# High and low activations side by side in one 512-column product, and a filter product that contracts over all 128 rows

## The chip, the cores and the metric

The kernel runs on one core of a Trainium2 chip. The core has five engines that run side by side and wait for each other by semaphores: TensorE (PE, matrix products into the PSUM banks; its weight loads are a row of their own, PEld), VectorE (DVE), ScalarE (ACT), GpSimd (POOL, which does not reach PSUM) and SyncE (SP, which issues the DMAs). The metric is device time of one execution in microseconds (us), lower is better.

## The reference

Two layers of an encoder trunk on one sequence of 256 tokens of width 1024, all in float32. Shortened to what the products are:

```python
for l in range(DEPTH):                                  # DEPTH = 2
    u = rms_norm(x, norm_mix_pre[l])
    proj = u @ w_in[l]                                  # [q,k,v: 4608 columns | Hyena v,x1,x2: 3072 columns]
    y_att = dilated_attention(q, k, v) @ w_o_attn[l]
    hv, hx1, hx2 = split(short_conv(proj[..., 4608:], conv_w, conv_b), 3)
    filt = implicit_filters(...)                        # (sin MLP @ w3) * decay
    z = hx1 * bidir_fft_conv(hv, filt[0], filt[1], hy_bias[0])
    z = hx2 * bidir_fft_conv(z, filt[2], filt[3], hy_bias[1])
    y_hy = z @ w_o_hyena[l]
    gates = sigmoid(u @ w_gate[l] + b_gate[l])          # 2 x 1024 columns
    x = x + rms_norm((gates0 * y_att + gates1 * y_hy) @ w_out[l], norm_mix_post[l])
    u = rms_norm(x, norm_ffn_pre[l])
    a, b = split(u @ w_gate_up[l], 2)                   # 2 x 2816 columns
    x = x + rms_norm((silu(a) * b) @ w_down[l], norm_ffn_post[l])
```

## The kernel before

Weights stream in as pieces of 128 rows of SBUF by 768 or 1024 float32 values, in one fixed order (`order`). Every piece is split into a high and a low part (`whi`, `wlo`): ACT copies the rounded value (`hi_of`, L86), DVE or, for every fifth piece, POOL subtracts it (`lo_of`, L89). Activations are split in the same way. A float32 product is then three passes that add up in one PSUM bank: high weights by high activations, high by low, low by high (`mm3`, L80 to L83). `piece()` keeps three pieces split ahead of the one in use.

A layer's products come in this order: queries, keys and values of the head slots 0 and 1 by rows (384 columns a matmul); 24 Hyena column pieces (`col_proj`, then `shortconv`); 16 gate pieces (`col_proj`, then a sigmoid); head slots 2 and 3; 8 pieces of `w_o_hyena` and 4 of `w_o_attn` (their results are multiplied by the gates, L750 and L766, and the sum is split into `MH`, `ML`); `w_out` by rows (`row_proj`); then the FFN: 8 pieces by rows, 38 by columns (`col_proj`, `Silu`, product, L794 to L800), and `w_down` by rows. `col_proj` runs eight blocks `k` of 128 rows, each an `mm3` with 256 columns (all tokens).

The three by-columns kinds of product have their activations in two tiles each: `UH`, `UL` for u, `zh`, `zl` for the Hyena result, `OTH`, `OTL` for attention.

Beside the pieces runs side work, in generators that `tick()` advances one step after each piece: the filters (`filter_chunk`, 16 of them, eight for a layer: `sd`, `sh`, `sl`, then two pairs of products with `gst`, then `dd`, `dl` and the transforms into `K`), attention (`attend`) and the convolutions (`conv`). `gst` holds 128 rows: the high part of 64 values above the low part of the same 64; the weights `w3` stand twice, in rows 0 to 63 and 64 to 127.

The order on PE is the order in which the code is written. On ACT, DVE, POOL and SP a scheduler sets the order when the program is built, except in the stretches marked `ordered()` between phases. PSUM has eight banks of 512 float32 columns, all in one ring (`acc`).

Of the kernel before, what the change touches and what calls it, by code (L numbers as in the profile page):

```python
# [39 lines left out]
# piece numbers in the packed weights  # L40
# [4 lines left out]
def trunk(tc, nc, a, out):  # L45
# [4 lines left out]
    with es:  # L50
# [82 lines left out]
        shared = [True]  # Pool takes some of the splitting  # L133
        count = [0, 0]  # pieces in wp; pieces split
# [95 lines left out]
        def sine(o, pre, n, par, c0):  # L230
            """o = sin(fr * (pre + b)), the argument brought into [-pi, pi] first."""
# [34 lines left out]
        def new_filter(l):  # L266
            """Tiles of the two filters' spectra and the jobs that fill them."""
# [14 lines left out]
        def filter_chunk(l, v, cc, K, fd, shared):  # L282
# [14 lines left out]
            late = l == 1 and cc == 2  # queued ahead of the layer's start, not to run in it  # L297
# [7 lines left out]
            lo_of(sl[:64], sd[:64], sh[:64], nc.gpsimd)  # L305
# [3 lines left out]
            for e in range(2):  # L309
                h = acc()  # L310
                mm(h, gst[l][:, e, :], sh, True, False)
                mm(h, gst[l][0:64, e, :], sl[0:64], False, True)
# [11 lines left out]
            for s in range(2):  # cosine transform of the sum, sine transform of the difference  # L324
# [45 lines left out]
        def add_to_x(i, t, r):  # L370
            """x += rms_norm * gain for one token tile."""
# [20 lines left out]
        def to_cols(i, u, U):  # L392
            """The transpose of one token tile of u, in parts."""
            for h in range(2):
# [27 lines left out]
        def rows_of(U, o, i, pc, kk, n):
            """Two of the eight row blocks of u[tile i] @ w for a piece of n columns."""
# [82 lines left out]
        def start(U, second, at=0):  # L506
            """The first 2 * 384 columns of a phase by rows, the first token tile ahead of the second."""
# [452 lines left out]
```

## Time and profile before

| | |
|---|---|
| runs | 1122.82 us median of 3 (1122.39 to 1125.14) |
| span of the profiled execution | 1117.8 us, first to last instruction; the median of the runs is 5.0 us above it |
| busy | PE 1094.3 us (98%), PEld 1035.3, DVE 704.1 (63%), ACT 557.1 (50%), POOL 412.5 (37%) |
| matmuls | 7624 in the trace, each with a weight load of its own |
| transfers | 187.21 MB, mean 167 GB/s |

Matmuls are pipelined and the end of one is modelled, so that PE's busy time says only that a matmul was under way; how much one costs is read from the distance between the starts of two. The profile's times are counted from the start of its span. In the trace the layer-0 mixer reaches to about 370 us, its FFN to about 575, the layer-1 mixer to about 918 and its FFN to the end.

### The profile page before, as it was taken

The numbers are of one execution on the slowest core, as the hardware profiler recorded it, in microseconds if no ns is written. First come the engines' busy times: TensorE is split into PE (matmuls) and PEld (weight loads), VectorE is DVE, ScalarE is ACT, GpSimd is POOL, SyncE is SP. The second block draws the span as 40 slices with busy tenths as digits, with TensorE's granted clock in tenths as the row PEclk, the third lists the DMA queues.
The fourth block names the chain that finished last, engine by engine and source line by source line (L and its number), as shares of the span: only waits on it lengthen the run. The fifth ranks groups of instructions, "written<-read, shape, count | busy, mean of one in ns | idle before, by whom it ended". The sixth has DMA issues, their size and how long they took to land.

```text
span 1117.8 us, 19545 instructions
## 1 busy us (share of the span) xinstructions
PE 1094.3 (98%) x7624; PEld 1035.3 (93%) x7624; DVE 704.1 (63%) x1128; ACT 557.1 (50%) x852; POOL 412.5 (37%) x499
## 2 busy tenths in 40 slices
PE   8999999999999999999999999999999999999997
PEld 7889999999998899999879899999999978999986
DVE  6789875556557756665474877865545676454554
ACT  6555564444645644454455564454355455544442
POOL 3665133468614224211125714455645221111110
PEclk9999999999999999999999999999999999999999
DMA  8565534444545655555655444444355466456662
GB/s 295 170 228 187 153 127 136 129 127 125 153 143 183 198 189 169 185 175 183 198 195 166 137 165 145 133 152 129 121 169 186 151 207 207 137 185 182 201 199 79
DMA packets 59878, 187.21 MB, mean 167 GB/s; under 512 B 6919, under 2 KB 9353, under 8 KB 59786
## 3 DMA queue, kind: packets, MB, share of 16 engines
q1 hardware_dynamic: 59786, 185.96, 52.1%
q8 instruction: 60, 0.98, 0.4%
q14 instruction: 32, 0.26, 0.1%
HBM read 184.89 MB, written 1.05 MB: 166 GB/s over the span
## 4 chain that ended last, share of the span: by engine, by line
PE 85%; DVE 5%; DMA 3%; POOL 2%; ACT 2%; issue 1%; SPq 0%; DVEq 0%; POOLq 0%; ACTq 0%
PE acc L78 83%; DVE wlo L89 2%; DMA gain<-in_gains_dram 1%; DMA raw<-in_wa_dram 1%; PE acc L617 1%; ACT whi L86 1%; ACT jk L352 1%; DVE X L373 1%; DMA raw<-in_wq_dram 1%; POOL GT L767 1%; PE acc L397 1%; PE acc L548 1%; PE acc L647 1%; POOL wlo L89 1%; DVE dd L315 0%
## 5 line engine op out<-in xcount | busy, mean ns | idle before, releaser
L86 ACT ACTIVATE whi<-raw 128x1024 fp32r<-128x1024 f32 (+1 forms) x352 | 345.4, 990 | 399.1 <-PE acc L78 297.4
L89 DVE TENSOR_TENSOR wlo<-raw,whi 128x1024 fp32r<-128x1024 f32 (+1 forms) x291 | 346.6, 1197 | 232.7 <-ACT whi L86 220.6
L78 PE MATMUL acc<-UH,whi 128*128 128x256 f32 x1248 | 357.6, 287 | 0.0
L78 PE MATMUL acc<-UH,wlo 128*128 128x256 f32 x1248 | 353.7, 283 | 0.0
L78 PE MATMUL acc<-UL,whi 128*128 128x256 f32 x1248 | 353.5, 283 | 0.0
L89 POOL TENSOR_TENSOR wlo<-raw,whi 128x1024 fp32r<-128x1024 f32 (+1 forms) x61 | 137.2, 2248 | 408.4 <-ACT whi L86 396.6
L78 PEld LDWEIGHTS acc<-UH,whi 128*128 128x128 f32 x1248 | 239.6, 192 | 2.5 <-issue 1.7
L78 PEld LDWEIGHTS acc<-UL,whi 128*128 128x128 f32 x1248 | 239.6, 192 | 0.0
L78 PEld LDWEIGHTS acc<-UH,wlo 128*128 128x128 f32 x1248 | 239.5, 192 | 0.0
L78 PE MATMUL acc<-wlo,UH 128*128 128x384 f32 x448 | 152.3, 340 | 6.0 <-DVE wlo L89 3.8
L78 PE MATMUL acc<-whi,UH 128*128 128x384 f32 x448 | 153.6, 343 | 0.0
L78 PE MATMUL acc<-whi,UL 128*128 128x384 f32 x448 | 150.8, 337 | 0.0
L78 PE MATMUL acc<-whi,hs 128*128 128x512 f32 x352 | 109.1, 390 | 0.0
L78 PEld LDWEIGHTS acc<-wlo,UH 128*128 128x128 f32 x448 | 84.8, 189 | 10.6 <-DVE wlo L89 6.9
L78 PEld LDWEIGHTS acc<-whi,UH 128*128 128x128 f32 x448 | 84.8, 189 | 2.0 <-issue 1.1
L78 PEld LDWEIGHTS acc<-whi,UL 128*128 128x128 f32 x448 | 84.6, 189 | 0.2 <-DVE UL L89 0.2
L78 PEld LDWEIGHTS acc<-whi,hs 128*128 128x128 f32 x352 | 66.1, 188 | 13.7
L78 PE MATMUL acc<-wlo,hs 128*128 128x512 f32 x176 | 68.7, 390 | 0.2 <-DVE wlo L89 0.2
L799 DVE TENSOR_TENSOR HF<-acc,silu 128x256 f32<-128x256 f32 x38 | 16.1, 424 | 52.5 <-PE acc L78 52.5
L359 POOL TENSOR_SCALAR nv<-ss 128x1 f32<-128x1 f32 x16 | 4.8, 300 | 107.5 <-ACT jk L352 107.5
L78 PEld LDWEIGHTS acc<-wlo,hs 128*128 128x128 f32 x176 | 33.1, 188 | 7.3 <-DVE wlo L89 0.7
L565 POOL TENSOR_TENSOR t<-t 128x256 f32<-128x256 f32 x32 | 23.5, 737 | 38.9 <-DVE t L562 38.0
(164 smaller groups left out, 1695.8 us busy)
## 6 DMA issues: line engine op xcount, KB each, us to landing
raw<-in_wa_dram SPq DMA_DIRECT2D x240, 512.0 KB, 3.6
raw<-in_wq_dram SPq DMA_DIRECT2D x96, 384.0 KB, 3.1
raw<-in_wg_dram SPq DMA_DIRECT2D x16, 384.0 KB, 4.4
w<-in_w_dram SPq DMA_DIRECT2D x16, 256.0 KB, 3.7
gain<-in_gains_dram SPq DMA_DIRECT2D x7, 512.0 KB, 7.0
dec<-in_dec_dram SPq DMA_DIRECT2D x8, 256.0 KB, 2.7
bb<-in_hyb_dram SPq DMA_DIRECT2D x16, 128.0 KB, 3.8
dftraw<-in_dft_dram SPq DMA_DIRECT2D x3, 256.0 KB, 4.5
```

The costliest lines, as they stand in the source:

```text
L78: nc.tensor.matmul(o, lT, r, start=start, stop=stop)
L86: return nc.scalar.activation(o, i, AF.Copy)
L89: (eng or nc.vector).tensor_tensor(o, i, h, op=OP.subtract)
L352: nc.scalar.activation(jk, half, AF.Square, scale=D ** -0.5, accum_out=ss[:, h:h + 1])
L373: stt(X[i][:, HALF[h]], t[h], r, X[i][:, HALF[h]], op0=OP.mult, op1=OP.add)
L397: nc.tensor.transpose(t[:, q * P:(q + 1) * P], u[:, h * 512 + q * P: h * 512 + (q + 1) * P], ident)
L548: nc.tensor.transpose(t[:, q * P:(q + 1) * P], eo[:, q // 2, q % 2, :], ident)
L565: ptt(t1[:, 0:256], t1[:, 0:256], t1[:, 256:512], op=OP.subtract)
L617: nc.tensor.transpose(t[:, q * P:(q + 1) * P], qk[i][:, j * 384 + g * P: j * 384 + (g + 1) * P], ident)
L647: nc.tensor.transpose(t[:, q * P:(q + 1) * P], S[:, i * 512 + q * P:i * 512 + (q + 1) * P], ident)
L767: ptt(g0, g0, ct(GT, 8 + c), op=OP.add)
L799: vtt(ct(HF, f), ob, sl, op=OP.mult)
```

## The change

The high and low activations of one block now stand side by side in one tile (`U`, `Z`, `OT`). `wide` replaces `mm3` for the products by columns: one matmul of the high weights with all 512 columns (high and low), then one of the low weights with the 256 high columns, into the first half of the bank. `halves` adds the two halves of the bank: ACT copies the second half to SBUF, DVE adds the first half to it. So the short convolution, the sigmoid, the silu and the gate products now read from SBUF what they read from PSUM. The FFN's product of the two columns and the gate product of the Hyena output move from DVE to POOL; `to_cols` splits a transposed tile in four parts of 256 columns instead of two of 512. In the filters the low part `sl` is made and contracted over 128 rows instead of 64. Comments are removed, so line numbers after the change are other ones.

```diff
-            lo_of(sl[:64], sd[:64], sh[:64], nc.gpsimd)
+            lo_of(sl, sd, sh, nc.gpsimd)
...
                 mm(h, gst[l][:, e, :], sh, True, False)
-                mm(h, gst[l][0:64, e, :], sl[0:64], False, True)
+                mm(h, gst[l][:, e, :], sl, False, True)
...
-                uh, ul = (x[:, i * 512:(i + 1) * 512] for x in U[h])
-                hi_of(uh, t)
-                lo_of(ul, t, uh)
+                for q in range(2):
+                    uh, ul = (U[2 * h + q][:, w + i * 256:w + (i + 1) * 256] for w in (0, 512))
+                    hi_of(uh, t[:, q * 256:(q + 1) * 256])
+                    lo_of(ul, t[:, q * 256:(q + 1) * 256], uh)
...
+        def wide(o, wh, wl, both, start, stop):
+            mm(o, wh, both, start, False)
+            mm(o[:, :L], wl, both[:, 0], False, stop)
+
+        def halves(y, o):
+            nc.scalar.activation(y, o[:, L:], AF.Copy)
+            vtt(y, o[:, :L], y, op=OP.add)
...
-        def col_proj(U):
+        def col_proj(U, y):
...
-            o = acc()[:, :L]
+            o = acc()
             for k in range(KT):
                 s = slice(k * P, (k + 1) * P)
-                mm3(o, wh[:, s], wl[:, s], *u_cols(U, k), k == 0, k == KT - 1)
+                wide(o, wh[:, s], wl[:, s], u_cols(U, k), k == 0, k == KT - 1)
             done(pc)
-            return o
+            halves(y, o)
+            return y
...
-        def shortconv(l, y, u, c):
+        def shortconv(l, y, U, c):
+            u = col_proj(U, sm.tile([P, L], F32, tag="hs", bufs=5, name="uc"))
...
-                nc.scalar.activation(ct(GT, c), col_proj(U), AF.Sigmoid, bias=bgt[:, l, c:c + 1])
+                g = col_proj(U, ct(GT, c))
+                nc.scalar.activation(g, g, AF.Sigmoid, bias=bgt[:, l, c:c + 1])
...
-                    mm3(o[:, :L], wh[:, s], wl[:, s], ct(ZH, k), ct(ZL, k), k == 0, k == KT - 1)
+                    wide(o, wh[:, s], wl[:, s], parts(Z, k), k == 0, k == KT - 1)
                 done(pc)
-                vtt(ct(GT, 8 + c), ct(GT, 8 + c), o[:, :L], op=OP.mult)
+                y = sm.tile([P, L], F32, tag="hs", bufs=5, name="yh")
+                halves(y, o)
+                ptt(ct(GT, 8 + c), ct(GT, 8 + c), y, op=OP.mult)
...
-                    mm3(o[:, :L], wh[:, s], wl[:, s], ct([OT[0]], k), ct([OT[1]], k), k == 0, k == 3)
+                    wide(o, wh[:, s], wl[:, s], parts(OT, k), k == 0, k == 3)
                 if c % 2:
                     done(pc)
+                y = sm.tile([P, L], F32, tag="hs", bufs=5, name="ya")
+                halves(y, o)
                 g0 = ct(GT, c)
-                vtt(g0, g0, o[:, :L], op=OP.mult)
+                vtt(g0, g0, y, op=OP.mult)
...
-                oa, ob = col_proj(U), col_proj(U)
-                sl = f256("silu")
-                nc.scalar.activation(sl, oa, AF.Silu)
-                vtt(ct(HF, f), ob, sl, op=OP.mult)
+                sl = col_proj(U, f256("silu"))
+                nc.scalar.activation(sl, sl, AF.Silu)
+                hf = col_proj(U, ct(HF, f))
+                ptt(hf, hf, sl, op=OP.mult)
```

PE, in the Hyena pieces of layer 0 around a filter chunk. Before:

```order
L78 MATMUL acc<-UH,whi 128x256
L78 MATMUL acc<-UL,whi 128x256
L78 MATMUL acc<-UH,wlo 128x256
L78 MATMUL acc<-sh,gst_96 128x512
L78 MATMUL acc<-sl,gst_96 128x512
L78 MATMUL acc<-sh,gst_96 128x512
L78 MATMUL acc<-sl,gst_96 128x512
L78 MATMUL acc<-UH,whi 128x256
L78 MATMUL acc<-UL,whi 128x256
L78 MATMUL acc<-UH,wlo 128x256
```

PE at the same place after the change:

```order
L78 MATMUL acc<-U,whi 128x512
L78 MATMUL acc<-U,wlo 128x256
L78 MATMUL acc<-sh,gst_96 128x512
L78 MATMUL acc<-sl,gst_96 128x512
L78 MATMUL acc<-sh,gst_96 128x512
L78 MATMUL acc<-sl,gst_96 128x512
L78 MATMUL acc<-U,whi 128x512
L78 MATMUL acc<-U,wlo 128x256
```

Three matmuls of a block have become two; the four of the filter chunk stand where they stood (the size shown is that of the output).

DVE in the Hyena pieces of layer 0, from the split of one piece to that of the next (`X` is a column tile of the short convolution, `dd` the filters'). Before:

```order
L89 TENSOR_TENSOR wlo<-raw,whi 128x1024
L590 SCALAR_TENSOR_TENSOR X_932<-acc,cw,X_932 128x192
L591 SCALAR_TENSOR_TENSOR X_932<-acc,cw,X_932 128x192
L315 TENSOR_TENSOR dd<-acc,dec 128x256 x2
L592 SCALAR_TENSOR_TENSOR X_932<-acc,cw,X_932 128x63
L593 SCALAR_TENSOR_TENSOR X_932<-acc,cw,X_932 128x63
L315 TENSOR_TENSOR dd<-acc,dec 128x256 x2
L89 TENSOR_TENSOR wlo<-raw,whi 128x1024
```

DVE after the change (`uc` is the SBUF tile of the product):

```order
L89 TENSOR_TENSOR wlo<-raw,whi 128x1024
L420 TENSOR_TENSOR uc<-acc,uc 128x256
L607 SCALAR_TENSOR_TENSOR X_938<-uc,cw,X_938 128x192
L608 SCALAR_TENSOR_TENSOR X_938<-uc,cw,X_938 128x192
L610 SCALAR_TENSOR_TENSOR X_938<-uc,cw,X_938 128x63
L315 TENSOR_TENSOR dd<-acc,dec 128x256 x2
L609 SCALAR_TENSOR_TENSOR X_938<-uc,cw,X_938 128x63
L315 TENSOR_TENSOR dd<-acc,dec 128x256 x2
L89 TENSOR_TENSOR wlo<-raw,whi 128x1024
```

One addition a piece has come in, and the four instructions of the short convolution have both tensors in SBUF.

DVE at the end of the layer-0 mixer, in the products with `w_o_attn` (`GT` is a gate, `ML` the low part of the merged columns). Before:

```order
L766 TENSOR_TENSOR GT<-GT,acc 128x256 x2
L89 TENSOR_TENSOR wlo<-raw,whi 128x1024
L766 TENSOR_TENSOR GT<-GT,acc 128x256
L89 TENSOR_TENSOR ML<-GT,MH 128x256
L766 TENSOR_TENSOR GT<-GT,acc 128x256
L89 TENSOR_TENSOR ML<-GT,MH 128x256
L89 TENSOR_TENSOR wlo<-raw,whi 128x1024
```

DVE there after the change (`ya` is the SBUF tile of the product):

```order
L420 TENSOR_TENSOR ya<-acc,ya 128x256
L788 TENSOR_TENSOR GT<-GT,ya 128x256
L89 TENSOR_TENSOR wlo<-raw,whi 128x1024
L420 TENSOR_TENSOR ya<-acc,ya 128x256 x2
L788 TENSOR_TENSOR GT<-GT,ya 128x256
L89 TENSOR_TENSOR ML<-GT,MH 128x256
L788 TENSOR_TENSOR GT<-GT,ya 128x256
L89 TENSOR_TENSOR wlo<-raw,whi 128x1024
```

Eight additions have come in between the splits of the next pieces, and the gate products read `ya` from SBUF.

## Rows read from the trace of the kernel before

**Rows 1.** The profile's page: busy time of each engine with its share of the span and its instructions, and the shares of the span of the chain that ended last, by engine.

```profile
PE 1094.3 (98%) x7624; PEld 1035.3 (93%) x7624; DVE 704.1 (63%) x1128; ACT 557.1 (50%) x852; POOL 412.5 (37%) x499
...
PE 85%; DVE 5%; DMA 3%; POOL 2%; ACT 2%; issue 1%; SPq 0%; DVEq 0%; POOLq 0%; ACTq 0%
```

**Rows 2.** Timeline of PE in the FFN columns of layer 1: start in us, duration, engine, line, operation, output<-inputs, shape. The first and the last of a row of 25 matmuls of 256 columns without a gap.

```profile
1000.00 0.28 PE L78 MATMUL acc<-UH,whi 128*128 128x256 f32 x1
...
1002.88 0.28 PE L78 MATMUL acc<-UH,whi 128*128 128x256 f32 x1
```

**Rows 3.** Timeline of the weight loads (PEld) in the same stretch: the load for a matmul that starts at 1000.12.

```profile
1000.00 0.19 PEld L78 LDWEIGHTS acc<-UL,whi 128*128 128x128 f32 x1
```

**Rows 4.** Timeline of PE in the last product by rows: the first and the last of 20 matmuls of 512 columns without a gap.

```profile
1079.62 0.39 PE L78 MATMUL acc<-wlo,hs 128*128 128x512 f32 x1
...
1083.92 0.39 PE L78 MATMUL acc<-whi,hs 128*128 128x512 f32 x1
```

**Rows 5.** Stretches of the span: length in us, busy us (instructions) of PE, PEld, DVE, ACT and POOL, granted clock of PE, share of the DMA engines, GB/s.

```profile
75.00:140.00 65.00, 65.00 (x487) 59.64 (x488) 59.40 (x138) 35.05 (x53) 23.41 (x16) 1.00 0.59 183
...
643.00:740.00 97.00, 97.00 (x812) 96.75 (x810) 74.76 (x166) 50.51 (x77) 36.61 (x37) 1.00 0.45 148
...
954.00:1050.00 96.00, 96.00 (x802) 96.00 (x801) 46.60 (x56) 44.36 (x66) 16.85 (x7) 1.00 0.58 181
```

**Rows 6.** The chain that ended last, in order of time: start us, length us, what. Where it comes to PE in layer 0 ahead of the Hyena pieces; where it leaves PE and comes back at the end of the layer-0 mixer; and the same at the start of layer 1.

```profile
74.49 64.72 PE acc L78 x479
...
336.68 1.07 ACT whi L86
...
370.01 0.66 PE acc L397 x4
...
609.33 0.48 DVE wlo L89
...
618.84 24.18 PE acc L78 x136
```

**Rows 7.** Groups of instructions of one line, kind and shape over the whole span, PE: count, then busy us, mean ns of one, and idle time before them.

```profile
L78 PE MATMUL acc<-UH,whi 128*128 128x256 f32 x1248 | 357.6, 287 | 0.0
...
L78 PE MATMUL acc<-zh,whi 128*128 128x256 f32 x128 | 37.1, 290 | 0.0
...
L78 PE MATMUL acc<-OTH,whi 128*128 128x256 f32 x64 | 18.1, 283 | 0.0
...
L78 PE MATMUL acc<-sl,gst 64*128 64x512 f32 x32 | 15.9, 497 | 1.9 <-POOL sl L89 1.9
```

**Rows 8.** Timeline of the weight loads (PEld) at a filter chunk of layer 0; in brackets the idle time before.

```profile
79.06 0.18 PEld L78 LDWEIGHTS acc<-sl,gst 64*128 64x128 f32 x1 [0.24 <-issue]
```

**Rows 9.** Timeline of PE at the same chunk (the second `sh`, `sl` pair left out).

```profile
78.74 0.39 PE L78 MATMUL acc<-sh,gst 128*128 128x512 f32 x1
79.06 0.49 PE L78 MATMUL acc<-sl,gst 64*128 64x512 f32 x1
...
80.34 0.39 PE L78 MATMUL acc<-UH,whi 128*128 128x256 f32 x1
80.56 0.28 PE L78 MATMUL acc<-UL,whi 128*128 128x256 f32 x1
```

**Rows 10.** Groups by form over the whole span: the nearest kinds to what the change adds (a copy of 256 columns from PSUM on ACT, and two sizes of SCALAR_TENSOR_TENSOR on DVE with both tensors in SBUF).

```profile
L334 ACT ACTIVATE ev<-acc 128x256 f32<-128x256 f32 x16 | 6.0, 376 | 2.6 <-PE acc L78 2.5
...
L241 DVE SCALAR_TENSOR_TENSOR arg<-kk,arg 128x256 f32<-128x256 f32 x6 | 2.6, 438 | 0.2
...
L385 DVE SCALAR_TENSOR_TENSOR u<-X,nr,gain 128x512 f32<-128x512 f32 x12 | 8.5, 748 | 2.9 <-POOL nr L360 2.9
```

**Rows 11.** Timeline of DVE under two splits of weights that POOL runs: under the first the first two of nine instructions that read PSUM, and the last; under the second the one instruction with both inputs in SBUF.

```profile
84.62 0.40 DVE L591 SCALAR_TENSOR_TENSOR hv<-acc,cw,hv 128x192 f32<-128x192 f32 x1
84.95 0.41 DVE L332 TENSOR_TENSOR ev<-acc,bb 128x256 f32<-128x256 f32 x1
...
86.98 0.40 DVE L591 SCALAR_TENSOR_TENSOR hv<-acc,cw,hv 128x192 f32<-128x192 f32 x1
...
478.47 2.21 DVE L89 TENSOR_TENSOR dl<-dd,dh 128x512 fp32r<-128x512 f32 x1 [2.14 <-ACT dh L86]
```

**Rows 12.** Timeline of POOL: the two splits of weights.

```profile
84.58 2.41 POOL L89 TENSOR_TENSOR wlo<-raw,whi 128x1024 fp32r<-128x1024 f32 x1 [0.43 <-ACT whi L86]
...
477.72 2.41 POOL L89 TENSOR_TENSOR wlo<-raw,whi 128x1024 fp32r<-128x1024 f32 x1 [12.31 <-ACT whi L86]
```

**Rows 13.** Groups of DVE by form in the stretch from 75 to 140 us.

```profile
L89 DVE TENSOR_TENSOR wlo<-raw,whi 128x1024 fp32r<-128x1024 f32 x14 | 18.7, 1339 | 1.0 <-ACT whi L86 1.0
...
L590 DVE SCALAR_TENSOR_TENSOR X<-acc,cw,X 128x192 f32<-128x192 f32 x9 | 3.7, 411 | 0.0
...
L590 DVE SCALAR_TENSOR_TENSOR hv<-acc,cw,hv 128x192 f32<-128x192 f32 x6 | 2.5, 408 | 0.0
...
L592 DVE SCALAR_TENSOR_TENSOR X<-acc,cw,X 128x63 f32<-128x63 f32 x8 | 2.2, 278 | 0.1
```

**Rows 14.** Groups of PE by form in the same stretch.

```profile
L78 PE MATMUL acc<-sl,gst 64*128 64x512 f32 x11 | 5.5, 496 | 0.0
```

**Rows 15.** Timeline of DVE at the end of the layer-0 mixer: the first and the last of 18 instructions from the first split of a `w_out` piece to the last `ML`.

```profile
340.65 1.35 DVE L89 TENSOR_TENSOR wlo<-raw,whi 128x1024 fp32r<-128x1024 f32 x1 [0.55 <-ACT whi L86]
...
352.81 0.42 DVE L89 TENSOR_TENSOR ML<-GT,MH 128x256 fp32r<-128x256 f32 x1 [0.20 <-ACT MH L86]
```

More of the change, by code (lines that the diff above doesn't have):

```diff
@@ L397, in to_cols @@
                     nc.tensor.transpose(t[:, q * P:(q + 1) * P], u[:, h * 512 + q * P: h * 512 + (q + 1) * P], ident)
-                uh, ul = (x[:, i * 512:(i + 1) * 512] for x in U[h])
-                hi_of(uh, t)
-                lo_of(ul, t, uh)
+                for q in range(2):
+                    uh, ul = (U[2 * h + q][:, w + i * 256:w + (i + 1) * 256] for w in (0, 512))
+                    hi_of(uh, t[:, q * 256:(q + 1) * 256])
+                    lo_of(ul, t[:, q * 256:(q + 1) * 256], uh)
         def new_U():
-            return [(bigt(F32R, name="UH"), bigt(F32R, name="UL")) for h in range(2)]
+            return [bigt(F32R, name="U") for h in range(4)]
         def u_cols(U, k, i=None):
-            vs = [x[:, :].rearrange("p (i k n) -> p i k n", i=2, k=4) for x in U[k // 4]]
-            return [v[:, :, k % 4, :] if i is None else v[:, i, k % 4, :] for v in vs]
-        def col_proj(U):
+            v = U[k // 2][:, :].rearrange("p (q i k n) -> p q i k n", q=2, i=2, k=2)
+            return v[:, :, :, k % 2, :] if i is None else (v[:, 0, i, k % 2, :], v[:, 1, i, k % 2, :])
+        def wide(o, wh, wl, both, start, stop):
[5 more added lines that the diff above has]
+        def col_proj(U, y):
             pc = piece()
             wh, wl = pc[:2]
-            o = acc()[:, :L]
+            o = acc()
             for k in range(KT):
                 s = slice(k * P, (k + 1) * P)
-                mm3(o, wh[:, s], wl[:, s], *u_cols(U, k), k == 0, k == KT - 1)
+                wide(o, wh[:, s], wl[:, s], u_cols(U, k), k == 0, k == KT - 1)
             done(pc)
-            return o
+            halves(y, o)
+            return y
         def rows_of(U, o, i, pc, kk, n):
@@ L531, in ct, with parts @@
             return T[c // 4][:, (c % 4) * L:(c % 4 + n) * L]
+        def parts(T, c):
+            return T[c // 2][:, (c % 2) * 512:(c % 2) * 512 + 512].rearrange("p (q n) -> p q n", q=2)
         def fold(z):
@@ L659, in attend @@
                     mm(op[:, i * P:(i + 1) * P], vt[:, w], PT[:, i * 512 + b * P:i * 512 + (b + 1) * P], b == 0, b == 3)
-            w = slice(s * L, (s + 1) * L)
-            hi_of(OT[0][:, w], op[:, :L])
-            lo_of(OT[1][:, w], op[:, :L], OT[0][:, w])
+            w = parts(OT, s)
+            hi_of(w[:, 0], op[:, :L])
+            lo_of(w[:, 1], op[:, :L], w[:, 0])
             yield
@@ L677, in mixer @@
                     qkv_out(j, i, o[j][i], qk, None)
-            OT = bigt(F32R, name="OTH"), bigt(F32R, name="OTL")
+            OT = [bigt(F32R, name="OT") for _ in range(2)]
             def slot(s, qk, then=None):
@@ L710, in mixer @@
                         c = 2 * cc + q
-                        shortconv(l, ct(T, c) if T else hv[:, q * L:(q + 1) * L], col_proj(U), c0 + c)
+                        shortconv(l, ct(T, c) if T else hv[:, q * L:(q + 1) * L], U, c0 + c)
                         tick()
@@ L724, in mixer @@
             for c in range(16):
-                nc.scalar.activation(ct(GT, c), col_proj(U), AF.Sigmoid, bias=bgt[:, l, c:c + 1])
+                g = col_proj(U, ct(GT, c))
+                nc.scalar.activation(g, g, AF.Sigmoid, bias=bgt[:, l, c:c + 1])
                 tick()
-            ZH, ZL = [], []
+            Z = []
             def z_split():
-                for h in range(2):
-                    zh, zl = bigt(F32R, name="zh"), bigt(F32R, name="zl")
-                    hi_of(zh, X2[h])
-                    lo_of(zl, X2[h], zh)
-                    ZH.append(zh)
-                    ZL.append(zl)
+                for c in range(0, 8, 2):
+                    Z.append(bigt(F32R, name="Z"))
+                    zh, zl = (Z[-1][:, :].rearrange("p (c q n) -> p c q n", c=2, q=2)[:, :, q] for q in range(2))
+                    x = ct(X2, c, 2).rearrange("p (c n) -> p c n", c=2)
+                    hi_of(zh, x)
+                    lo_of(zl, x, zh)
             for s in (2, 3):
```

## The prediction

> **What bounds the kernel now.** I read the page first. PE is busy for 98% of the span, and 85% of the chain that ended last is PE; DVE follows with 63% busy [rows 1]. A busy PE need not be a PE at its pace, so the distance between starts came next. In the FFN columns 24 matmuls of 256 columns take 2.88 us, 120 ns each [rows 2], and the weight load of the next one starts while the one before it runs: that for the matmul at 1000.12 starts at 1000.00 [rows 3]. In the product by rows, 19 matmuls of 512 columns take 4.30 us, 226.3 ns each [rows 4]. The difference of 106.3 ns for 256 columns leaves 13.7 ns that a matmul costs beside its columns. The granted clock is the full one of 2.4 GHz (1.00) in every stretch shown [rows 5]. So PE is the bound nearly everywhere, and one matmul less at the same number of columns is worth 13.7 ns. The exceptions are where the chain is off PE: it comes to PE for a long run only at 74.5 us, and leaves it from 336.7 to 370.0 and from 609.3 to 618.8 [rows 6] for splits, transfers and filters; the layer-1 mixer has a twin of the second. What PE saves there is waited away.
>
> **The wide products.** A block of 128 rows has been three matmuls of 256 columns (360.0 ns) and becomes one of 512 and one of 256 (226.3 + 120.0 = 346.3): 13.7 ns less. The groups count 1248 + 128 + 64 = 1440 blocks [rows 7], so PE gives up 1440 x 13.7 ns = 19.7 us, while the columns stay the same.
>
> The Trainium skill, "TensorE: Matmul & The Clock Gate", section "Wait — 56ns, not 53.3ns?", has only some 2.5 ns as the fixed cost of a matmul at the full clock. By that the wide products would save an estimated 3.6 us (1440 x 2.5 ns). The rows of this kernel show 13.7 ns, at both sizes.
>
> **The filter product.** At a filter chunk the matmul with `sl` has 64 rows and the one before it 128. Its weight load starts at 79.06, together with its own matmul and after an idle 0.24 us of the loader [rows 8], not one matmul earlier as in [rows 3]; so does each of the four loads up to the first of the next product. From 78.74 to the second matmul of the next product at 80.56 pass 1.82 us [rows 9]; four of 512 columns and one of 256 at the pace of the other rows are 4 x 0.226 + 0.120 = 1.025. That is 0.80 us a chunk, and 32 such products [rows 7] are 16 chunks: 12.8 us. With 128 rows everywhere I expect the loads to go ahead like all the others.
>
> The Trainium skill speaks against this edit: the same page, Part 3, section "The mechanism", has weight loads overlap running matmuls "only when row_grp differs", so that two full sets of rows would not overlap and the edit would win nothing (the 12.8 us would stay). The trace shows 128-row loads under 128-row matmuls throughout, and the 64-row ones waiting.
>
> PE's part is thus 19.7 + 12.8 = 32.5 us of the profiled span of 1117.8. The median of the runs lies 5.0 above that span, and I carry this over.
>
> **What the sum of the halves costs.** The code has 188 wide products (172 of eight blocks and 16 of four: 1440), each with one copy on ACT (376 ns [rows 10]) and one DVE addition with one input in PSUM. DVE instructions of this kind take 0.40 us but start 0.33 apart [rows 11], so one costs 0.33. Over the whole span that is 71 us on ACT and 62 on DVE; 54 products with gates and silu leave DVE for POOL. Where DVE and ACT are half idle this lies under PE: in the FFN columns of layer 1 DVE is busy 46.6 of 96 us, ACT 44.4, POOL 16.9 [rows 5]. There the FFN's 19 products on POOL cannot cost more than a split of 1024 columns each (2.41 us [rows 12]), 46 us in 79 free. Without this cover each product would add 0.38 + 0.33 = 0.71 us. I price FFN, gates and `w_o_hyena` at nothing.
>
> The four short-convolution instructions now read SBUF alone. Now they take 0.41 us (192 columns) and 0.28 (63) [rows 13]. With both tensors in SBUF the same instruction takes 438 ns at 256 columns and 748 at 512 [rows 10]; on that line 192 columns are 0.36 and 63 are 0.20, together 0.25 us less for a product. The bounds are 0 and 0.25; I take half, 0.12.
>
> What isn't in a price list is the wait for POOL. Under a POOL split of 2.41 us nine DVE instructions with an input in PSUM run at their usual 0.40, five of them the short convolution's; one with both inputs in SBUF (512 columns) that starts at 478.47 under the other split takes 2.21 us and ends at 480.68, 0.55 after that split [rows 11, 12]: it waited for POOL to finish and then did its work. The short convolution joins the second kind. I bound what that costs a stretch by nothing and by all the time that POOL is busy there, and take a third.
>
> - Layer 0, 75 to 140 us. 15 Hyena products fall here (9 + 6 [rows 13]) and five of the layer's eight filter chunks (eleven products with `sl` [rows 14], the first of them of a chunk that began before). PE saves 15 x 8 x 13.7 ns + 5 x 0.80 = 5.6 us, to 59.4. DVE is busy 59.4 of 65 already [rows 5]; it gets 15 x (0.33 - 0.12) = 3.2 and a third of POOL's 23.4, 7.8 (bounds 0 and 23.4): 70.4. DVE becomes the bound and the stretch takes 70.4 us instead of 65: the 5.6 us are lost and 5.4 more, 11.0 given back (bounds 0 and 27).
> - Layer 1, 643 to 740 us. PE saves 24 x 8 x 13.7 ns = 2.6, to 94.4. DVE has 74.8 [rows 5], gets 24 x 0.21 = 5 and a third of 36.6, 12: 92. That is just below PE; I give back 2 (bounds 0 and 10).
> - The other three chunks of layer 0 start ahead of 75 us, where the chain is not PE's; I count two of them as lost, 1.6. At the start of layer 1 (609.3 to 618.8) another two: 1.6.
> - End of the mixer. From 340.65 to 352.81 us DVE goes through 18 instructions nearly without a gap [rows 15], the chain passes through them to the transfer of the gains and reaches PE again at 370.0 [rows 6]. Eight additions (2.7 us) come in, and the gate products now have both inputs in SBUF beside POOL's additions. Queued behind them on DVE are `ML` and the splits of `w_out`, and behind those, by the buffers they free, the loads and the gains on SP's queue, which the first norm waits for. I take 3.5 us a layer, 7.0 in all (bounds 0 and 12). The same chain would hide any PE gain in it.
>
> Twice two splits of 256 columns instead of one of 512 in `to_cols` let the first product start earlier and the last one later; I price that at nothing, as both stand in front of the same 16 transposes.
>
> **Sum.** 32.5 - 11.0 - 2 - 1.6 - 1.6 - 7.0 = 9.3 us. The profiled span becomes 1108.5, the median 1113.5.
>
> **Rivals.** A measurement of this kernel tells about 0.3% (3.4 us) from no change.
>
> - All of PE's gain lands but what the chain hides in front (chance 0.24). DVE's order was set anew, and its instructions with PSUM inputs (additions, `dd`, `K`) could stand under POOL's splits, as they do now [rows 11, 12]. Then 1122.8 - 32.5 + 3.2 + some 3 to 10 at the mixer's end: 1096 to 1104. Against it: DVE at 91% in 75 to 140 [rows 5].
> - The waits for POOL eat it all (0.15): half of POOL's busy time instead of a third in both Hyena stretches makes DVE's work 74.3 us in the first (14.9 given back) and 98 in the second (3.7), with 9 at the mixers' ends: 1122.8 - 32.5 + 3.2 + 14.9 + 3.7 + 9 = 1121. No change.
> - DVE becomes the bound of the Hyena stretches and the kernel slower (0.12). Place: the short convolution beside POOL's splits and filters. Price: from half of POOL's time on, every further tenth adds 2.3 us in layer 0 and 3.7 in layer 1; at four fifths that is 18 more, 1139. It decides from about 0.6 on.
> - PE does not become cheaper (0.06). The 512-column matmul alternates with one of 256, which no row here shows; if its pace came to the old 360 ns a block, 19.7 us would be missing: 1133. If the 128-row loads waited as now, 12.8 would be: 1126. The Trainium skill's fixed cost and its rule on row groups, both cited above, are nearest to these two.
>
> The forecast itself, 1104 to 1119, has 0.43. **Range.** From the best rival's end, 1097, to 1131, which leaves out the far part of the slower cases; the forecast's own range is 1104 to 1119. Faster by over 0.3% (below 1119.4): 0.43 + 0.24 = 0.67; within 0.3%: 0.15; slower: 0.12 + 0.06 = 0.18.
>
> **What would show it.** The 512-column and the 256-column matmul of a block start 226 and 120 ns apart; four filter matmuls and their successor in 1.03 us, loads ahead of them; 6184 matmuls instead of 7624. In 75 to 140 us PE has gaps ended by DVE (`wlo`, `dl` or `uc`), and short-convolution instructions of 1 us and more stand under POOL's splits. At the mixer's end the chain from the last `w_o_attn` product to the transposes is longer than 33.3 us (336.7 to 370.0). The prediction is wrong if PE stays without gaps through the Hyena pieces (then the time is near 1098), or if DVE's waits for POOL there exceed 0.6 of POOL's busy time (then it is 1126 or more).

## The result and the profile after

The changed kernel takes 1133.57 us (median of 4 runs, 1130.44 to 1136.3) against 1123.7 us of the kernel before (4 runs, 1122.39 to 1125.14). The ratio is 1.0089, with a 95% interval of 1.0067 to 1.011: it is slower, where 1113.5 us had been forecast. The profiled execution has a span of 1132.2 us (before 1117.8; that execution was a quick one: the spans of the 13 timed runs of before beside e5 to e8 begin at 1119.6. So the two traces differ by 14.4 us and the medians by 9.9).

The page after: busy time, the granted clock in 40 slices, and the shares of the chain that ended last.

```profile
PE 1083.1 (96%) x6184; PEld 967.0 (85%) x6184; DVE 786.4 (69%) x1282; ACT 618.4 (55%) x1060; POOL 456.5 (40%) x553
...
PEclk9998899999999999999999999999999999999999
...
PE 72%; DVE 15%; DMA 4%; POOL 3%; issue 3%; ACT 2%; SPq 0%; DVEq 0%; POOLq 0%; ACTq 0%
```

Beside [rows 1]: 1440 matmuls are gone, and still PE's share of the chain has fallen from 85% to 72% while that of DVE has trebled. Two slices near the start are no longer at the full clock.

Where the time went is read from stages that both traces have. The table is in us, by starts of matmuls: the Hyena pieces from their first matmul to the first of the gates, gates and FFN columns from their first to their last; "mixer's end" is from the first product with `w_o_attn` to the first wide product of the FFN. The other rows are those of the experiments below.

| kernel | time, us (ratio to before) | Hyena pieces, layer 0 | Hyena, layer 1 | gates, layer 1 | FFN columns, layers 0, 1 | mixer's end, layers 0, 1 |
|---|---|---|---|---|---|---|
| before | 1123.7 | 97.7 | 90.7 | 60.1 | 122.5, 110.0 | 56.1, 56.1 |
| after | 1133.6 (1.0089) | 111.9 | 94.1 | 62.8 | 117.2, 107.7 | 58.5, 59.1 |
| e1 filters only | 1114.7 (0.9916) | 93.7 | 90.7 | 60.1 | 119.4, 109.9 | 57.3, 55.9 |
| e2 Hyena in three passes | 1110.1 (0.9869) | 93.7 | 90.7 | 59.5 | 117.2, 107.7 | 58.0, 58.1 |
| e3 sum in PSUM | 1110.7 (0.9874) | 97.0 | 88.9 | 59.5 | 117.2, 107.7 | 59.5, 58.2 |
| e4 no addition | 1108.4 (0.9856) | 92.3 | 88.9 | 59.5 | 117.2, 107.7 | 59.4, 58.2 |
| e5 widths grouped | 1103.6 (0.9814) | 93.7 | 90.7 | 59.4 | 116.1, 106.7 | 56.8, 57.2 |
| e6 attention output narrow | 1104.7 (0.9815) | 93.7 | 90.7 | 59.5 | 117.2, 107.7 | 56.6, 56.8 |
| e7 combined | 1099.2 (0.977) | 93.7 | 88.8 | 59.4 | 116.1, 106.7 | 56.0, 56.1 |
| e8 no splits on POOL | 1122.7 (0.9984) | 103.9 | 88.9 | 64.9 | 117.2, 107.7 | 57.9, 58.0 |

So PE's gain is there where nothing stands against it (FFN columns: 5.3 us in layer 0, 3.1 of them from the filters as e1 shows, and 2.3 in layer 1), and the loss is in the Hyena pieces, above all those of layer 0: 14.2 us. Stretches, columns as in [rows 5]. First the Hyena pieces of layer 0 in the trace before:

```profile
75.80:173.50 97.70, 97.70 (x766) 92.60 (x766) 83.25 (x199) 54.54 (x85) 32.33 (x26) 1.00 0.52 163
```

Then the trace after: the Hyena pieces of both layers, five microseconds inside the first, and the FFN columns of layer 1.

```profile
76.40:188.20 111.80, 99.45 (x573) 87.21 (x572) 104.56 (x223) 61.61 (x108) 32.20 (x26) 0.94 0.45 144
654.30:748.30 94.00, 90.76 (x570) 81.68 (x569) 86.73 (x174) 52.38 (x90) 35.93 (x37) 0.98 0.40 130
90.00:95.00 5.00, 4.18 (x16) 3.70 (x17) 5.00 (x9) 1.18 (x3) 2.98 (x4) 0.50 0.00 2
954.00:1050.00 96.00, 96.00 (x550) 84.00 (x549) 54.07 (x72) 54.00 (x95) 25.55 (x21) 1.00 0.58 187
```

In layer 0 DVE is busy 104.56 of 111.8 us (83.25 of 97.7 before) and PE has gaps; for a while the granted clock is 0.50, that is 1.2 instead of 2.4 GHz. In the FFN columns PE has no gap and the full clock, as in [rows 5].

How it comes about is seen in eight microseconds. DVE in the timeline after, at the same place as the first part of [rows 11]:

```profile
84.14 2.62 DVE L608 SCALAR_TENSOR_TENSOR hv<-uc,cw,hv 128x192 f32<-128x192 f32 x1
86.69 0.27 DVE L610 SCALAR_TENSOR_TENSOR hv<-uc,cw,hv 128x63 f32<-128x63 f32 x1
86.88 0.41 DVE L420 TENSOR_TENSOR uc<-acc,uc 128x256 f32<-128x256 f32 x1
...
87.87 0.81 DVE L609 SCALAR_TENSOR_TENSOR hv<-uc,cw,hv 128x63 f32<-128x63 f32 x1
88.61 1.23 DVE L89 TENSOR_TENSOR dl<-dd,dh 128x512 fp32r<-128x512 f32 x1
...
90.42 1.24 DVE L89 TENSOR_TENSOR dl<-dd,dh 128x512 fp32r<-128x512 f32 x1
91.58 1.42 DVE L607 SCALAR_TENSOR_TENSOR hv<-uc,cw,hv 128x192 f32<-128x192 f32 x1
```

POOL in the same stretch (a split of weights, the filters' sums and their low part):

```profile
84.14 2.40 POOL L89 TENSOR_TENSOR wlo<-raw,whi 128x1024 fp32r<-128x1024 f32 x1 [6.42 <-PE acc L78]
87.87 0.73 POOL L296 TENSOR_TENSOR sd<-w 128x256 f32<-128x256 f32 x1 [1.33 <-DMA w<-in_w_dram]
...
91.07 1.72 POOL L89 TENSOR_TENSOR sl<-sd,sh 128x512 fp32r<-128x512 f32 x1
```

And PE behind both:

```profile
87.03 0.28 PE L78 MATMUL acc<-U,wlo 128*128 128x256 f32 x1
87.15 0.28 PE L78 MATMUL acc<-dh,fd 128*128 128x256 f32 x1
89.89 0.58 PE L78 MATMUL acc<-dl,fd 128*128 128x256 f32 x1 [2.46 <-DVE dl L89]
...
94.87 0.63 PE L78 MATMUL acc<-U,whi 128*128 128x512 f32 x1
95.29 0.41 PE L78 MATMUL acc<-U,wlo 128*128 128x256 f32 x1
95.51 0.63 PE L78 MATMUL acc<-U,whi 128*128 128x512 f32 x1
...
96.61 0.40 PE L78 MATMUL acc<-U,whi 128*128 128x512 f32 x1
96.84 0.28 PE L78 MATMUL acc<-U,wlo 128*128 128x256 f32 x1
96.96 0.39 PE L78 MATMUL acc<-U,whi 128*128 128x512 f32 x1
```

An instruction of the short convolution that takes 0.41 us by itself starts together with POOL's split of 2.40 us and takes 2.62. The filters' `dl` stands behind it on DVE; PE stands in front of `dl` for 2.46 us. Then the clock falls: the pair of a wide block takes 95.51 - 94.87 = 0.64 us until about 96.2, and 0.35 after that. The waits of PE in the whole trace (us in total, times, longest) mostly name the same engine:

```profile
PE acc L78 <- DVE dl L89: 11.5, 6, 3.2
PE acc L78 <- DVE wlo L89: 7.4, 11, 1.5
PE acc L397 <- DVE u L385: 6.7, 4, 2.5
...
PE acc L78 <- DVE nl L89: 3.2, 1, 3.2
```

All six waits for `dl` lie in the Hyena pieces of layer 0.

### The profile page after: what moved, and what is told of

Same layout as the page of the kernel before. It is cut to its first block, busy times and chain, and to the rows that moved or that the text cites. A ratio compares the mean times of both kernels' runs of the same rounds, so it can differ in the third digit from the quotient of the medians.

```text
span 1132.2 us, 17177 instructions
## 1 busy us (share of the span) xinstructions
PE 1083.1 (96%) x6184; PEld 967.0 (85%) x6184; DVE 786.4 (69%) x1282; ACT 618.4 (55%) x1060; POOL 456.5 (40%) x553
## 4 chain that ended last, share of the span: by engine, by line
PE 72%; DVE 15%; DMA 4%; POOL 3%; issue 3%; ACT 2%; SPq 0%; DVEq 0%; POOLq 0%; ACTq 0%
PE acc L78 70%; DVE wlo L89 4%; DMA gain<-in_gains_dram 2%; DMA raw<-in_wq_dram 1%; DVE X L609 1%; DVE dl L89 1%; DVE X L608 1%; ACT whi L86 1%; DVE X L373 1%; DVE uc L420 1%; ACT jk L352 1%; PE acc L634 1%; DVE hv L608 1%; DVE GT L788 1%; POOL wlo L89 1%
## 5 line engine op out<-in xcount | busy, mean ns | idle before, releaser
L78 PE MATMUL acc<-U,whi 128*128 128x512 f32 x1248 | 448.8, 402 | 0.0
L78 PE MATMUL acc<-U,wlo 128*128 128x256 f32 x1248 | 351.5, 282 | 0.0
L78 PEld LDWEIGHTS acc<-U,whi 128*128 128x128 f32 x1248 | 236.8, 190 | 55.1
L78 PE MATMUL acc<-whi,U 128*128 128x384 f32 x896 | 238.9, 339 | 0.8 <-ACT whi L86 0.8
L78 PEld LDWEIGHTS acc<-U,wlo 128*128 128x128 f32 x1248 | 237.9, 191 | 0.4
L78 PEld LDWEIGHTS acc<-whi,U 128*128 128x128 f32 x896 | 163.8, 189 | 2.4 <-ACT whi L86 1.2
L78 PE MATMUL acc<-wlo,U 128*128 128x384 f32 x448 | 152.4, 340 | 6.5 <-DVE wlo L89 4.5
L78 PEld LDWEIGHTS acc<-wlo,U 128*128 128x128 f32 x448 | 84.7, 189 | 11.7 <-DVE wlo L89 8.2
L78 PE MATMUL acc<-Z,whi 128*128 128x512 f32 x128 | 46.3, 403 | 0.0
L89 DVE TENSOR_TENSOR hs<-HF,hs 128x256 fp32r<-128x256 f32 x44 | 36.2, 839 | 10.4 <-ACT hs L86 10.4
L581 POOL TENSOR_TENSOR t<-t 128x256 f32<-128x256 f32 x32 | 23.7, 745 | 43.9 <-DVE t L578 43.3
```

Source lines behind the costliest of these rows:

```text
L78: nc.tensor.matmul(o, lT, r, start=start, stop=stop)
L89: (eng or nc.vector).tensor_tensor(o, i, h, op=OP.subtract)
L581: ptt(t1[:, 0:256], t1[:, 0:256], t1[:, 256:512], op=OP.subtract)
```

## Experiments

Two theories stood against each other at first. Theory 1: the short convolution waits for POOL, because both its tensors now lie in SBUF. Theory 2: the work that was added (a copy and an addition for each product) fills DVE.

**e1, the filter edit alone.** Before, and only the two lines of the filters.

```diff
-            lo_of(sl[:64], sd[:64], sh[:64], nc.gpsimd)
+            lo_of(sl, sd, sh, nc.gpsimd)
...
-                mm(h, gst[l][0:64, e, :], sl[0:64], False, True)
+                mm(h, gst[l][:, e, :], sl, False, True)
```

> The kernel before with the filter edit alone (sl made and contracted over 128 rows). The wide products are absent. By the prediction's working a chunk loses 0.80 us on PE, 12.8 us in all, and 3.2 of them are hidden behind other engines: about 9 to 10 us faster than before, some 1113 us. If the saved PE time only turns into waits for DVE's dl in the stretch from 75 to 140 us, it is 5 us or less.

Measured: 1114.66 us (1114.31 to 1117.0), ratio 0.9916 (0.9892 to 0.994): 9.6 us faster than the 1124.23 of before beside it. It is the changed kernel's good half; what the wide products bring with them costs some 19 us on top of it (1133.6 against 1114.7).

**e2, the Hyena products in three passes.** After, but the 48 Hyena products go back to three matmuls of 256 columns, and the short convolution reads PSUM (`col_three` is the old loop of `mm3`, without the sum of the halves).

```diff
-            u = col_proj(U, sm.tile([P, L], F32, tag="hs", bufs=5, name="uc"))
+            u = col_three(U)
```

> The changed kernel with the Hyena columns alone as they were before (three matmuls of 256 columns a block, the short convolution reads PSUM); gates, FFN, w_o_hyena, w_o_attn and the filters as changed. If the Hyena stretches are the whole loss, they take again what they took before or less (99.0 and 92.1 us, against 114.5 and 98.9 in the changed kernel) and the kernel is at 1106 to 1112 us. If the loss is spread over all wide products, it stays above 1120.

**e3, the sum written back to PSUM.** After, with the wide product, the copy and the addition all kept; only the place of the sum is another (`halves` written out).

```diff
-            vtt(y, o[:, :L], y, op=OP.add)
-            return y
+            vtt(o[:, :L], o[:, :L], y, op=OP.add)
+            return o[:, :L]
```

> The changed kernel, but in the Hyena columns the sum of the two halves is written back to PSUM, so that the short convolution has one input in PSUM as before. Count and size of the instructions on DVE, ACT and PE are those of the changed kernel. Theory 1 (the short convolution waits for POOL because both its tensors lie in SBUF): the waits go, the first Hyena stretch falls from 114.5 to about 103 us and the kernel to 1113 to 1120. Theory 2 (the 48 additions and the longer way over ACT and DVE are too much work for DVE there, wherever the tensors lie): no change, 1129 to 1134.

**e4, as e3 without the addition.**

```diff
-            vtt(o[:, :L], o[:, :L], y, op=OP.add)
             return o[:, :L]
```

> As the run with the sum in PSUM, but the addition of the halves is left out in the Hyena columns (the copy on ACT stays): the short convolution reads the first half alone, so the product of high weights by low activations is left out of the Hyena columns. It prices the 48 additions. Theory 1: within 4 us of the run with the sum in PSUM. Theory 2: at least 8 us below it, about 1112 or less, as 48 x 0.33 = 16 us of DVE go.

Measured: e2 1110.05 us (1107.12 to 1112.54), ratio 0.9869 (0.9844 to 0.9895); e3 1110.67 us (1108.71 to 1111.72), ratio 0.9874 (0.9854 to 0.9894); e4 1108.42 us (1106.72 to 1110.4), ratio 0.9856 (0.9835 to 0.9878). e3 issues on every engine as many instructions as the changed kernel and is 23 us faster; taking the additions away as well (e4) brings 2 more, 4.7 in the Hyena pieces of layer 0 alone (97.0 to 92.3). Theory 2 falls as the cause of the loss, theory 1 stands. (The expectations of e2 and e3 count the Hyena stretches between other marks: their 114.5 and 98.9 us are the 111.9 and 94.1 of the table.) The Hyena pieces of layer 0 in e3, columns as above; DVE is busy 91.09 us there, and the clock stays at 1.00:

```profile
76.60:173.60 97.00, 93.38 (x574) 82.64 (x573) 91.09 (x223) 60.87 (x108) 32.09 (x26) 1.00 0.53 166
```

DVE of e3 at the place shown above:

```profile
84.41 0.41 DVE L622 SCALAR_TENSOR_TENSOR hv<-acc,cw,hv 128x192 f32<-128x192 f32 x1
84.73 0.42 DVE L445 TENSOR_TENSOR acc<-acc,uc 128x256 f32<-128x256 f32 x1
85.06 0.41 DVE L337 TENSOR_TENSOR K<-acc,ev 128x256 f32<-128x256 f32 x1
```

and POOL of e3:

```profile
84.41 2.41 POOL L89 TENSOR_TENSOR wlo<-raw,whi 128x1024 fp32r<-128x1024 f32 x1 [6.41 <-PE acc L78]
```

The same instruction under the same split takes 0.41 instead of 2.62 us. The sums over the Hyena pieces of layer 0, groups of DVE after:

```profile
L608 DVE SCALAR_TENSOR_TENSOR X<-uc,cw,X 128x192 f32<-128x192 f32 x15 | 10.4, 696 | 0.2
L609 DVE SCALAR_TENSOR_TENSOR X<-uc,cw,X 128x63 f32<-128x63 f32 x15 | 9.4, 625 | 0.0
L607 DVE SCALAR_TENSOR_TENSOR X<-uc,cw,X 128x192 f32<-128x192 f32 x15 | 6.3, 418 | 1.1 <-ACT X L606 1.0
```

and of e3:

```profile
L622 DVE SCALAR_TENSOR_TENSOR X<-acc,cw,X 128x192 f32<-128x192 f32 x15 | 6.2, 414 | 0.3
L623 DVE SCALAR_TENSOR_TENSOR X<-acc,cw,X 128x63 f32<-128x63 f32 x15 | 4.1, 276 | 0.2
```

The mean of L608 and L609 is far above that of their twins. All eight groups of the short convolution together take 45.8 us there in the trace after and 31.7 in the trace before: 14.1 us of waiting, 0.44 of POOL's 32.20 busy us; in layer 1 it is 15.2 us (84 instructions at their means, less the same at the means of before), 0.42 of 35.93. The Trainium skill, "SBUF — State Buffer", section "Who interferes with whom", has it so: a DVE instruction with two SBUF inputs contends with a GpSimd one that reads SBUF, and one with at most one SBUF input, outside the modes that it calls 2-port, does not. Both halves agree with these traces (2.62 us after, 0.41 in e3).

**e8, the same from POOL's side.** After, with no splits of weights on POOL in the two Hyena stretches; their 10 splits go to DVE.

```diff
+            shared[0] = False
             for cc in range(4):
                 hv = t512("hv")
...
+            shared[0] = True
             GT = [bigt(name="GT") for h in range(4)]
```

> The changed kernel (1133.6 us), but in the two Hyena stretches DVE does all splits of weights, so the 10 that POOL did (2.4 to 2.5 us each) become 10 more DVE instructions of 1.22 us, 12 us of work on the engine that is the bound. Theory 1, the short convolution's instructions are held by POOL's instructions while both of their tensors lie in SBUF: each POOL split cost DVE about 2.1 us of waiting, 21 us against 12, and the Hyena stretch of layer 0 falls from 111.9 us to 105 to 108, the time to 1124 to 1130 us. Theory 2, DVE's own added work fills the stretch: 6 us more in layer 0 and 4 in layer 1, 1140 to 1145 us.

Measured: 1122.68 us (1120.24 to 1126.23, 10 runs), ratio 0.9984 (0.9969 to 1.0). More work on the busiest engine made the kernel 11 us faster than the changed one, a little more than expected. The two Hyena stretches, columns as above:

```profile
77.30:181.20 103.90, 96.29 (x573) 84.90 (x572) 98.44 (x228) 61.72 (x108) 20.97 (x21) 0.97 0.49 155
645.10:734.00 88.90, 88.90 (x572) 80.07 (x570) 81.94 (x174) 52.37 (x91) 25.75 (x32) 1.00 0.40 137
```

DVE does 10 more splits and is busy for less time (98.44 against 104.56 and 81.94 against 86.73). What is left in layer 0 over e4's 92.3 us stands beside the additions (4.7 us by e3 and e4), POOL's other instructions (20.97 us: `sd`, `sl`, `eo`) and the splits that DVE now does; how much is which of the last two was not tried. The gates of layer 1 are longer than in the changed kernel (64.9 us against 62.8): PE waits there 2.5 us for a POOL instruction of the convolutions (`t`), and the clock is 0.97 in the mean.

**e5, the two widths in groups.** e2, and in each wide product all matmuls of 512 columns come before all of 256. The loop with `wide` written out:

```diff
-            for k in range(KT):
-                mm(o, wh(k), both(k), k == 0, False)
-                mm(o[:, :L], wl(k), both(k)[:, 0], False, k == KT - 1)
+            for k in range(KT):
+                mm(o, wh(k), both(k), k == 0, False)
+            for k in range(KT):
+                mm(o[:, :L], wl(k), both(k)[:, 0], False, k == KT - 1)
```

> The kernel with three narrow passes in the Hyena columns (1110.05 us), and every wide product issues its 512-column matmuls of all row blocks first and then its 256-column ones, instead of the two widths by turns; 1056 blocks. Theory 1, the pair costs 352 ns because the two widths alternate: the pitches return to 226.3 and 120.0 ns [rows 2, 4], 5.7 ns less for a block, 6.0 us less in all: 1103 to 1105 us. Rival, a matmul costs what it costs whatever stands next to it and the 226.3 ns of the filter's matmuls come from something else there: pitches near 235 and 117 ns remain, 1109 to 1111 us.

Measured: 1103.61 us (1102.81 to 1105.57), ratio 0.9814 (0.9798 to 0.983). The time is what theory 1 gave, the reason only in part, so that the agreement is in part luck. PE in the FFN columns of layer 1 after, the first and the last of 15 matmuls by turns:

```profile
1000.15 0.40 PE L78 MATMUL acc<-U,whi 128*128 128x512 f32 x1
...
1002.62 0.40 PE L78 MATMUL acc<-U,whi 128*128 128x512 f32 x1
```

and in e5, one product and the start of the next:

```profile
1001.55 2.00 PE L78 MATMUL acc<-U,whi 128*128 128x512 f32 x8
1003.39 1.11 PE L78 MATMUL acc<-U,wlo 128*128 128x256 f32 x8
1004.34 2.00 PE L78 MATMUL acc<-U,whi 128*128 128x512 f32 x8
```

By turns seven blocks take 2.47 us, 353 ns each. Grouped, eight take 1.84 + 0.95 = 2.79 us, 349 ns: 230 for the wide matmul and 119 for the narrow one, not the 226.3 of [rows 4]. The FFN columns became 1.1 and 1.0 us shorter, 3.5 ns for each of their 304 blocks; for all 1056 blocks that is 3.7 us. The mixers' ends give 2.1 more by the traces (58.0 and 58.1 to 56.8 and 57.2), of which the pace explains 0.2; why the order shortens those, no run here tells. Why a wide matmul takes 230 to 235 ns here stays open. Products of `U` read their activations in four pieces of 128 columns, those of `OT` in one piece of 512, and the pace is no better there; PE in e5 in the products with `w_o_attn`:

```profile
338.21 1.09 PE L78 MATMUL acc<-OT,whi 128*128 128x512 f32 x4
339.14 0.63 PE L78 MATMUL acc<-OT,wlo 128*128 128x256 f32 x4
```

Four wide matmuls take 0.93 us, 233 ns each, so the slower pace is there without the four pieces too.

**e6, the attention output narrow.** e2, and the eight products with `w_o_attn` ahead of the mixer's last projection are three passes again, their gate product reading PSUM.

```diff
-                    wide(o, wh[:, s], wl[:, s], parts(OT, k), k == 0, k == 3)
+                    both = parts(OT, k)
+                    mm3(o[:, :L], wh[:, s], wl[:, s], both[:, 0], both[:, 1], k == 0, k == 3)
...
-                halves(y, o)
-                vtt(g0, g0, y, op=OP.mult)
+                vtt(g0, g0, o[:, :L], op=OP.mult)
```

> The kernel with three narrow passes in the Hyena columns (1110.05 us), and the attention output (eight products ahead of the mixer's last projection) is back at three 256-column passes too, its gate product reading PSUM. Theory 1, the mixer's end is longer because a sum, a copy and a wait stand between the last product and the first matmul that needs it: the stretch from the first to the last matmul that reads MH goes back from 25.9 to about 23.7 us in each layer, the products cost 0.5 us more, and the time falls to 1105 to 1107 us. Rival, the stretch is longer because of something else (the output projection's weights or the norms): it stays near 26 us and the time is 1110 to 1111 us.

Measured: 1104.66 us (1102.83 to 1105.88), ratio 0.9815 (0.9798 to 0.9833). The stretch of the expectation, from the first to the last matmul that reads `MH`, falls from 26.3 us in both layers of e2 to 24.5 and 24.7, and the mixer's end from 58.0 and 58.1 to 56.6 and 56.8. That is 2.7 us by the traces, while the medians differ by 5.4; e2 ran on another chip, and the intervals of the two ratios leave room for either. The chip does not make the shorter stretch: e8, on e6's chip and with the attention output as changed, has 57.9 and 58.0. Theory 1 holds: taking the sum away shortens the stretch, and the price lies between these two. The sum is not all of it, as e5 keeps it and has 24.9 and 25.3 us.

**e7, all of it.** Filters over 128 rows; wide products in groups for gates, Hyena output and FFN; narrow ones for the attention output and layer 0's Hyena; layer 1's Hyena wide, in groups too, with the sum in PSUM.

> Filters over 128 rows; wide products, grouped by width, in the gates, the Hyena output and the FFN; three narrow passes in the attention output and in layer 0's Hyena columns; in layer 1's Hyena columns wide products whose sum goes back to PSUM. If the prices add up, it takes the gain of each of the others: from 1110.05 us 6 for the grouping, 4 for the mixers' ends and 2 to 3 for layer 1: 1096 to 1100 us. Rival, the gains overlap because the same waits end both: 1102 to 1106 us.

Measured: 1099.18 us (1097.14 to 1100.31), ratio 0.977 (0.9753 to 0.9787), faster than both kernels. The prices add up: FFN columns as in e5, layer 1's Hyena pieces as in e3, the mixers' ends at 56.0 and 56.1 as before the change. The chain that ended last:

```profile
PE 83%; DMA 4%; DVE 4%; POOL 3%; ACT 2%; issue 2%; SPq 0%; POOLq 0%; DVEq 0%; ACTq 0%
```

## Why the prediction was wrong

The prediction was wrong in its direction, and 1133.6 us is above its range. Two steps failed: the 11.0 and 2 us given back in the Hyena pieces, where DVE's sum of work was taken for the length of the stretch, and the 19.7 us of the wide products, which came to some 11. The traced span is 23.7 us longer than forecast (1132.2 against 1108.5). Against the prediction's terms, 9.8 us of that lie in layer 0's Hyena pieces (102.1 us by the terms), 8.4 in layer 1's and the gates behind them (90.1 and 58.4) and 4.0 in the FFN columns (115.1 and 105.8). Step by step:

- **The filter product: right.** 12.8 us less 3.2 hidden is 9.6, and e1 gave 9.6. That it fits to a tenth is luck, as e1's interval reaches from 6.7 to 12.1 us; the price of 0.80 a chunk is borne out by the stages (five chunks in the Hyena pieces of layer 0 gave 4.0 us, four in its FFN columns 3.1). The loads go ahead as expected; PE after, the first chunk's four matmuls and the next product's first,

```profile
79.13 0.39 PE L78 MATMUL acc<-sh,gst 128*128 128x512 f32 x1
79.36 0.40 PE L78 MATMUL acc<-sl,gst 128*128 128x512 f32 x1
...
80.05 0.39 PE L78 MATMUL acc<-U,whi 128*128 128x512 f32 x1
```

  and the load for `sl`, which starts with the matmul ahead of its own:

```profile
79.13 0.19 PEld L78 LDWEIGHTS acc<-sl,gst 128*128 128x128 f32 x1
```

  Four matmuls take 0.92 us, where the chunk of [rows 9] took 1.60 to the start of the next product (78.74 to 80.34). The rule of the Trainium skill ("TensorE: Matmul & The Clock Gate", Part 3, "The mechanism") that loads overlap only where the row group differs does not hold here as it stands; the same section also lets a load go ahead into a "background weight buffer", and no run here tells whether that is what happens.
- **The wide products: the mechanism right, the size not.** A block costs 353 ns instead of 346.3: 7 to 8 ns saved and not 13.7. The FFN columns of layer 1 show it undisturbed: 304 blocks, 110.0 to 107.7 us, 7.6 ns each. Over 1440 blocks that is some 11 us, 8 to 9 less than the term. The failed step is to take the pace of a 512-column matmul from a row where it stands among its like [rows 4] and put it beside a 256-column one; the prediction had this as a rival and priced its worst end alone. The alternation is only about half of it: in groups (e5) a block still takes 349 ns, and the rest stays open.
- **The short convolution from SBUF, 0.12 us cheaper a product: wrong.** Where no POOL instruction overlaps them, those of 192 columns have medians of 407 and 408 ns in the trace after and those of 63 columns 273 and 274 (before 411 and 278 [rows 13]): hardly cheaper. The line through two points of [rows 10] gave 360 ns at 192 columns. Only one of the points, L385 with 748 ns at 512, lies nearly on one line with the short convolution's 407 and 273; the other, L241, multiplies by a constant where these read a value for each partition, and whether that is why it lies lower no run tells.
- **The wait for POOL in the Hyena pieces: the mechanism right, the size and what follows from it wrong.** The waiting took 0.44 of POOL's time in layer 0 and 0.42 in layer 1, not a third; that by itself would be 2.5 us in the 65 us that were costed. The larger error is the step after it: the stretch was taken as long as DVE's sum of work, with DVE at 100% and PE at its old pace. But much of the waiting comes in pieces of some 2 us, right in front of what PE needs next (`dl` 11.5 us in six waits, one `nl` of 3.2), so PE stood although DVE still had 7 idle us in layer 0 and 7 in layer 1. With neither the waits for POOL nor the additions the Hyena pieces of layer 0 take 92.3 us (e4); of the 19.6 us more, 14.9 go with the place of the sum (e3) and 4.7 with the additions. Seen from PE they are 12.3 of waits (`dl` 11.5, `PT` 0.8) and 7.3 in which it worked longer, at most 6.7 of that by the lower clock (half of 13.3 us at 0.50). By the prediction's terms the stretch would have been 97.7 + 5.4 - 9 x 8 x 0.0137 = 102.1 us; it took 111.9. Layer 1 was to give back 2 us; against e3 it lost 5.2 in the Hyena pieces and 3.3 in the gates behind them, where the short convolution's last instructions still run and PE waits 2.0 us for POOL's `t`, which had waited for DVE.
- **The clock: missing.** Rows of the kernel before show 1.00 in all stretches [rows 5], and the prediction kept it there. After a gap of PE the trace shows 0.50 five times: from 89.7 to 96.2 and from 120.2 to 127.0 us, and for 3.4 us each from 727.8, 761.9 and 936.0, 23.5 us in all. A gap does not always bring it: one of 2.46 us that ends at 384.83 is followed by 1.00 (382 to 577 us), and one of 1.98 us ahead of attention's transposes in layer 0 by 1.00 in the trace after (316.7 to 320.1), but by 0.50 in e3 (303.4 to 306.8) and e5 (299.0 to 302.3). What it cost on its own was not tried; if PE had work all the time it is at most half of that, 12 us.
- **The mixers' ends: right.** The prediction's 3.5 us a layer, less 0.4 of PE's own gain there, is 3.1; the trace shows 2.4 and 3.0 (56.1 to 58.5 and 59.1). The place is the one named: PE waits for `u` 6.7 us instead of 1.9, and 3.3 in e6. The size is known to about 1 us only: e1, whose mixers' ends are those of before, has 57.3 and 55.9 us and waits 3.5 for `u`.
- **Work priced at nothing** in the FFN is hidden as said (in layer 1's gates the Hyena pieces' work covers it up): 954 to 1050 us has PE at 96.00 of 96.00 with DVE at 54.07, ACT 54.00 and POOL 25.55.
- **The rivals.** The slower one had the place and the mechanism, and 1126 to 1139 us; its point of decision, 0.6 of POOL's time, was too high, since it too went by DVE's sum. It had 0.12. The rival beside it put half of POOL's time at 1121 us; measured were 0.44 and 1133.6.

## What to carry to other kernels

Before a result is moved from PSUM to SBUF, look at what reads it and at what POOL does in that stretch: an instruction that had one tensor in SBUF and now has two can cost a whole POOL instruction more, and writing the sum back to PSUM avoids it at the same number of instructions (1133.6 to 1110.7 us). On the engine that feeds PE, don't cost waits as a sum to be spread over the stretch; ask which matmul stands behind the longest one, and reckon that a lower clock may follow such a gap. A saving on PE is taken from matmuls in the neighbourhood that they will have, and kept out of the stages where another engine ends last.

## What the runs showed of the hardware

- SCALAR_TENSOR_TENSOR with both tensors in SBUF costs about what it does with one in PSUM if no POOL instruction runs beside it: 407 to 408 ns at 192 columns, 273 to 274 at 63 (medians after; 411 and 278 before [rows 13]).
- An instruction of 0.41 us with both tensors in SBUF takes 2.62 us under a POOL split of 2.40; with one tensor in PSUM it keeps its 0.41.
- Matmuls of 512 and 256 columns by turns take 235 and 117 ns, in groups 230 and 119; alone they had taken 226.3 and 120 [rows 2, 4].
- After a gap of 2.46 us PE ran at 1.2 GHz for some 6.5 us, busy though it was for most of it; a wide block then takes 0.64 us instead of 0.35. After another gap of 2.46 us the clock stayed at 1.00.
